# Every second weight chunk of the recurrent mixers: remainder by a negated copy on ScalarE and an accumulating DMA from GpSimd, in place of a subtraction on VectorE

## The chip, the cores and the metric

The kernel runs on one core of one Trainium2 chip. The metric is the device time of one execution in microseconds (us). Of each kernel several executions are timed; one more is recorded by the profiler, and all views below are of that one. Engine names in the views: PE is TensorE, PEld its weight loads, DVE VectorE, ACT ScalarE, POOL GpSimd, SP the engine that issues most DMAs.

## What is computed

256 tokens of width 1024, in float32, go through two layers of a first block and one of a second block. A layer of the first block is a feed-forward network, a recurrent mixer, and another feed-forward network. The mixer, cut to what matters:

```
proj = (h @ w_in)                          # 1024 x 3592, in fp32 accuracy
hg_q, hg_f, hg_i, hg_g, gd_q, gd_k, gd_v, gd_z, gd_b, gd_a, rg_x, rg_gate = split(proj)
o_hg = hgrn2_chunked(q, 1.0 - f, hg_i, log(f))          # 4 heads
o_gd = gated_delta_chunked(cq, ck, cv, g, beta)         # 4 heads, a triangular solve per 128 tokens
o_rg = rg_lru(causal_depthwise_conv(rg_x)) * gelu(rg_gate)
x = x + concat(o_hg, o_gd, o_rg) @ w_out                # 1024 x 1024
```

The feed-forward networks are `(silu(h @ w_gate) * (h @ w_up)) @ w_down` with an inner width of 2816. The second block has retention, dilated attention and a third feed-forward part.

## The kernel before

**Weights in two parts.** Every matrix product is done in three matmuls of type float32r, on a high part and a remainder of both operands: high by high, high by remainder, remainder by high. The function `wchunk` brings a weight chunk of at most 256 x 512 numbers into the form [128 partitions, 2, n]: a DMA on SP's queue writes it to `raw`, ScalarE copies it to `wh` (a cast, L92), and VectorE subtracts `wh` from `raw` and writes the remainder `wl` (L93). The pool of `raw` has 4 buffers and that of `wh` and `wl` 3 each. So a load into a `raw` buffer waits until the subtraction four chunks earlier is done, and a cast waits until the matmuls of the chunk three earlier are done.

**Who reads the chunks.** `gemm_feat` (output features on partitions) uses a chunk in 24 matmuls with lines L184 (`wh` by the high part), L185 (`wh` by the remainder) and L186 (`wl`). `gemm_tok` uses one in 12 matmuls, with lines L140, L141 (`wl`) and L142. PE takes its instructions in the order in which they stand: a matmul on `wl` that is not there yet holds up all that stand behind it.

**The mixer.** `Mixer` runs twice (mixer 0 and mixer 1). It projects in the order rg, ba, k, hg, vg, v, q, z, 4 chunks each, and its last step `project` has 8 chunks of `w_out`. Between these products stand the recurrences: `delta_solve` (matmuls `sv`, L711, with small steps on VectorE and ScalarE between them), `hg_scores` (matmuls `hS`, L915), `delta_core`. Here chunks are counted as the program asks for them: mixer 0 has chunks #71 to #110, mixer 1 #251 to #290. Of mixer 0, rg is #71 to #74, ba #75 to #78 (260 columns), k #79 to #82, hg #83 to #86, z #99 to #102 (260 columns) and `project` #103 to #110. The convolution after k starts with `xp` (L622).

**The order of the work.** No order is written out by hand. A scheduler of the framework puts each engine's instructions in a row when the program is built, after its own model of their times; so a change in one helper moves other instructions too. GpSimd has little to do before: it fills some tiles with zeros and makes four small copies and two larger ones.

Of the kernel before, what the change touches and what calls it, by code (L numbers as in the profile page):

```python
# [7 lines left out]
F32 = mybir.dt.float32  # L8
# [3 lines left out]
ALU = mybir.AluOpType  # L12
# [11 lines left out]
class Weights:  # L24
# [3 lines left out]
    def __init__(self, dram, size):  # L28
        self.dram, self.size, self.parts, self.off = dram, size, [], 0
# [22 lines left out]
class Ctx:  # L52


    def __init__(self, tc, stack):
        self.tc = tc
        self.nc = tc.nc
        pool = lambda name, bufs, **k: stack.enter_context(tc.tile_pool(name=name, bufs=bufs, **k))
        self.const = pool("const", 1)
        self.keep = pool("keep", 1)  # L60
        self.raw = pool("raw", 4)
        self.wsp = pool("wsp", 3)
        self.w2p = pool("w2", 11)
        self.small = pool("small", 2)
        self.ps_mm = pool("ps_mm", 4, space=bass.MemoryType.PSUM)
        self.ps_x = pool("ps_x", 2, space=bass.MemoryType.PSUM)
        self.m4 = pool("m4", 3)
        self.rowp = pool("rowp", 2)
        self.ret = pool("ret", 4)
        self.n = 0  # L70
        self.nx = 0
        self.xtags = ("xa", "xb")
        nc = self.nc
        self.ones = self.const.tile([P, P], F32, name="ones")
        nc.vector.memset(self.ones, 1.0)
        self.ident = self.const.tile([P, P], F32, name="ident")
        nc.gpsimd.affine_select(self.ident, self.ones, pattern=[[-1, P]], compare_op=ALU.is_equal,
                                fill=0.0, base=0, channel_multiplier=1)
# [6 lines left out]
    def wchunk(self, w, k0, nkt, c0, n, room=None):  # L85
        nc = self.nc
        raw = self.raw.tile([P, KC, 512], F32, tag="raw", name=self.nm("raw"))[:, :nkt, :n]
        nc.sync.dma_start(raw, w.chunk(k0, nkt, c0, n))
        if room is None:
            room = tuple(self.wsp.tile([P, KC, 512], F32R, tag=i, name=self.nm(i)) for i in ("wh", "wl"))  # L90
        h, l = (a[:, :nkt, :n] for a in room)
        nc.scalar.copy(h, raw)  # L92
        nc.vector.tensor_tensor(l, raw, h.bitcast(F32), op=ALU.subtract)  # L93
        return h, l

    def mm_tile(self, name="mm"):
# [199 lines left out]
def hidden_split(c, hT, hc, f0, nb):  # L296

    k0 = f0 // P
    h, l = hT[k0 // 8]
    k0 %= 8  # L300
    c.split(h[:, k0:k0 + nb], l[:, k0:k0 + nb], hc)


def ffn(c, st, wT, wg, wu, wd, F):


    nc = c.nc
    xs, r = st.norm_T(wT)
    rbc = r_broadcast(c, r)
    rq = c.small.tile([P, 2], F32, tag="rr", name=c.nm("rr"))  # L310
    nc.vector.tensor_scalar(rq, r, 0.25, None, op0=ALU.mult)
    KF = F // P
    hT = [c.hT_tile(j) for j in range((KF + 7) // 8)]
    rb = bc(rbc.unsqueeze(1), [P, 2, S])
    for c0 in range(0, F, 512):
        n = min(512, F - c0)
        g = c.gemm_feat(xs, wg, 8, c0, n)
        gs = []
        for i in range(n // 256):
            gn, th = v2(c.w2("gn"), 2), v2(c.w2("th"), 2)  # L320
            nc.vector.tensor_tensor(gn, v2(g[i], 2), rb, op=ALU.mult)
            nc.scalar.activation(th, gn, AF.Tanh, scale=0.5)
            nc.vector.scalar_tensor_tensor(th, th, 1.0, gn, op0=ALU.add, op1=ALU.mult)
            gs.append(th)
        u = c.gemm_feat(xs, wu, 8, c0, n)
        for i in range(n // 256):
            nc.vector.tensor_tensor(gs[i], gs[i], v2(u[i], 2), op=ALU.mult)
            hidden_split(c, hT, gs[i], c0 + 256 * i, 2)
    for c0 in (0, 512):
        o = c.gemm_tok(hT, wd, 0, KF, c0, 512)  # L330
        for t in range(2):
            xx = st.x[:, t, c0:c0 + 512]
            nc.vector.scalar_tensor_tensor(xx, o[t], rq[:, t:t + 1], xx, op0=ALU.mult, op1=ALU.add)
# [40 lines left out]
def bc(ap, shape):  # L374
    return ap.broadcast_to(list(shape))
# [29 lines left out]
def load_cols(c, col, layout):  # L405
    t = c.const.tile([P, col.shape[1]], F32, name="colp")
    c.nc.scalar.dma_start(t, col)
    return {k: t[:, o:o + w] for k, (o, w) in layout.items()}
# [53 lines left out]
def load_consts(c, tab):  # L462
    t = c.keep.tile([P, CTAB], F32, tag="ctab", name="ctab")[:, :CONST_TAB.shape[1]]
    c.nc.sync.dma_start(t, tab)
    c.K = {n: t[:, o:o + w] for n, (o, w) in CONST_LAYOUT.items()}
    c.K["ident"] = c.ident
    c.seg = c.const.tile([P, 4, P], F32, name="seg")
    c.nc.vector.memset(c.seg, 1.0)
    c.nc.vector.memset(c.seg[:, :, 0:1], 0.0)


def r_broadcast(c, r):

    nc = c.nc
    ps = c.x_tile("rbc")
    for t in range(2):
        dg = c.small.tile([P, P], F32, tag="dg", name=c.nm("dg"))
        nc.vector.tensor_scalar(dg, c.ident, r[:, t:t + 1], None, op0=ALU.mult)
        nc.tensor.matmul(ps[:, t * P:(t + 1) * P], c.ones, dg, start=True, stop=True)
    o = c.small.tile([P, S], F32, tag="rbcs", name=c.nm("rbcs"))  # L480
    nc.scalar.copy(o, ps[:, :S])
    return o


def v2(ap, a):
    return ap.rearrange("p (a b) -> p a b", a=a)
# [967 lines left out]
def block_kernel(tc, a, layout):  # L1454
    with ExitStack() as stack:
        c = Ctx(tc, stack)
        nc = c.nc
        st = Stream(c, a["x"])
        cols = load_cols(c, a["col"], layout)
        for L in range(2):  # L1460
            wn = lambda n: cols[n][:, 8 * L:8 * L + 8]
            ffn(c, st, wn("norm_ffn1"), a["ffn1_gate"][L], a["ffn1_up"][L], a["ffn1_down"][L], D_FF)
            if L == 0:
                load_consts(c, a["tab"])
                prm = MixParams(c, cols, a, a)
                fq = c.const.tile([P, 9], F32, name="fq")
                o = TAB2_LAYOUT["invf"][0]
                nc.sync.dma_start(fq, a["tab2"][:, o:o + 9])
                rope = Rope(c, a["pos_row"], a["pos_col"], fq[:, 0:1], fq[:, 1:9])
            Mixer(c, st, prm, a["w_in"][L], a["w_out"][L], L)  # L1470
            ffn(c, st, wn("norm_ffn2"), a["ffn2_gate"][L], a["ffn2_up"][L], a["ffn2_down"][L], D_FF)
        Block2(c, st, prm, a, rope)

# [40 lines left out]
```

## Time and profile before

| what | value |
|---|---|
| time, median of 3 runs | 1794.52 us (1789.35 to 1795.16) |
| the profiled execution: its time, its span | 1796.44 us, 1794.7 us |
| mean granted clock of TensorE | 0.981 |
| busy over the span: PE, DVE, ACT, POOL | 1734.5, 1207.1, 892.3, 13.4 us |

The profiled execution's time is 1.7 us over its span, and 1.9 us over the median of the runs. PE is busy 97% of the span, but a busy PE can be one that runs at a lower clock; the granted clock of a stretch says so. VectorE's share is not even over the span: it is highest in the two mixers, from about 197 to 386 us and from about 766 to 947 us.

### The profile page before, as it was taken

The numbers are of one execution on the slowest core, as the hardware profiler recorded it, in microseconds if no ns is written. First come the engines' busy times: TensorE is split into PE (matmuls) and PEld (weight loads), VectorE is DVE, ScalarE is ACT, GpSimd is POOL, SyncE is SP. The second block draws the span as 40 slices with busy tenths as digits, with TensorE's granted clock in tenths as the row PEclk, the third lists the DMA queues.
The fourth block names the chain that finished last, engine by engine and source line by source line (L and its number), as shares of the span: only waits on it lengthen the run. The fifth ranks groups of instructions, "written<-read, shape, count | busy, mean of one in ns | idle before, by whom it ended". The sixth has DMA issues, their size and how long they took to land.

```text
span 1794.7 us, 28677 instructions
## 1 busy us (share of the span) xinstructions
PE 1734.5 (97%) x11296; PEld 1568.8 (87%) x11296; DVE 1207.1 (67%) x2181; ACT 892.3 (50%) x1352; POOL 13.4 (1%) x40
## 2 busy tenths in 40 slices
PE   8999989989999999989889999999999999999996
PEld 8997989879998999889879998888888788799885
DVE  6666689866655665589967665745666666766566
ACT  5444574444444444466345444555454544455454
POOL 0000000000000000000000000000000000000000
PEclk9999999899999999999989999999999999999998
DMA  6546542235565555543315556555443456645561
GB/s 233 186 153 220 163 135 84 94 104 185 176 197 189 183 188 181 186 151 118 127 47 177 187 169 199 185 176 173 133 130 124 146 176 211 200 155 198 194 229 53
DMA packets 91654, 292.38 MB, mean 163 GB/s; under 512 B 11008, under 2 KB 23808, under 8 KB 91520
## 3 DMA queue, kind: packets, MB, share of 16 engines
q1 hardware_dynamic: 91376, 290.45, 49.4%
q8 instruction: 88, 1.44, 0.3%
q14 instruction: 46, 0.38, 0.1%
q10 hardware_dynamic: 144, 0.11, 0.0%
HBM read 289.47 MB, written 1.05 MB: 162 GB/s over the span
## 4 chain that ended last, share of the span: by engine, by line
PE 90%; DVE 6%; ACT 2%; issue 1%; DMA 1%; SPq 0%; DVEq 0%; ACTq 0%
PE mm L185 13%; PE mm L186 13%; PE mm L184 13%; PE mm L140 13%; PE mm L141 13%; PE mm L142 13%; PE sv L711 2%; DVE wl L93 1%; ACT wh L92 1%; PE pv L1234 1%; PE dS L658 1%; PE dsc L1202 1%; PE hS L915 1%; PE dsc L1201 0%; DVE cv L630 0%
## 5 line engine op out<-in xcount | busy, mean ns | idle before, releaser
L93 DVE TENSOR_TENSOR wl<-raw,wh 128x1024 fp32r<-128x1024 f32 (+2 forms) x544 | 639.8, 1177 | 462.8 <-ACT wh L92 461.4
L92 ACT CAST wh<-raw 128x1024 fp32r<-128x1024 f32 (+2 forms) x544 | 549.3, 1011 | 652.1 <-PE mm L185 281.0
L184 PE MATMUL mm<-xTh,wh 128*128 128x256 f32 x2112 | 595.6, 284 | 13.1 <-DVE xp L622 10.0
L185 PE MATMUL mm<-xTl,wh 128*128 128x256 f32 x2112 | 598.0, 284 | 2.2 <-DVE xTl L197 2.1
L186 PE MATMUL mm<-xTh,wl 128*128 128x256 f32 x2112 | 595.2, 283 | 0.8 <-DVE wl L93 0.7
L184 PEld LDWEIGHTS mm<-xTh,wh 128*128 128x128 f32 x2112 | 401.4, 191 | 17.9 <-ACT th L572 10.4
L185 PEld LDWEIGHTS mm<-xTl,wh 128*128 128x128 f32 x2112 | 402.5, 191 | 4.7 <-DVE xTl L197 3.7
L186 PEld LDWEIGHTS mm<-xTh,wl 128*128 128x128 f32 x2112 | 403.0, 191 | 2.8 <-DVE wl L93 1.3
L141 PE MATMUL mm<-wl,hT 128*128 128x512 f32 x608 | 241.4, 398 | 2.4 <-DVE wl L93 2.4
L142 PE MATMUL mm<-wh,hT 128*128 128x512 f32 x608 | 238.8, 394 | 0.0
L140 PE MATMUL mm<-wh,hT 128*128 128x512 f32 x608 | 219.3, 397 | 4.8 <-DVE scr L573 4.8
L141 PE MATMUL mm<-wl,xTh 128*128 128x512 f32 (+1 forms) x440 | 169.3, 386 | 0.0
L142 PE MATMUL mm<-wh,xTl 128*128 128x512 f32 (+1 forms) x440 | 166.2, 380 | 0.0
L140 PE MATMUL mm<-wh,xTh 128*128 128x512 f32 (+1 forms) x440 | 160.2, 384 | 2.5 <-ACT xTh L196 2.5
L140 PEld LDWEIGHTS mm<-wh,hT 128*128 128x128 f32 x608 | 114.9, 190 | 30.2 <-DVE scr L573 5.2
L141 PEld LDWEIGHTS mm<-wl,hT 128*128 128x128 f32 x608 | 115.4, 190 | 28.3 <-DVE wl L93 3.9
L142 PEld LDWEIGHTS mm<-wh,hT 128*128 128x128 f32 x608 | 115.2, 189 | 24.7 <-DVE hT L197 0.2
L140 PEld LDWEIGHTS mm<-wh,xTh 128*128 128x128 f32 x440 | 82.0, 188 | 19.0 <-ACT xTh L196 2.9
L142 PEld LDWEIGHTS mm<-wh,xTl 128*128 128x128 f32 x440 | 83.0, 189 | 16.6 <-issue 2.0
L141 PEld LDWEIGHTS mm<-wl,xTh 128*128 128x128 f32 x440 | 82.9, 188 | 16.2 <-issue 1.9
L196 ACT ACTIVATE xTh<-xtr,colp 128x256 fp32r<-128x256 f32 (+1 forms) x72 | 28.9, 453 | 12.4 <-DVE xTl L197 12.3
L711 PE MATMUL sv<-hS,LTm 128*128 128x32 f32 x192 | 27.5, 293 | 7.3 <-ACT hS L732 4.3
(441 smaller groups left out, 1608.2 us busy)
## 6 DMA issues: line engine op xcount, KB each, us to landing
raw<-in_weights SPq DMA_DIRECT2D x514, 512.0 KB, 3.3
raw<-in_weights SPq DMA_DIRECT2D x32, 256.0 KB, 3.1
raw<-in_weights SPq DMA_DIRECT2D x16, 260.0 KB, 3.1
x_res<-in_x SPq DMA_DIRECT2D x2, 512.0 KB, 4.3
rowp<-in_b_gate SPq DMA_DIRECT2D x2, 512.0 KB, 4.8
out<-pg SPq DMA_DIRECT2D x4, 256.0 KB, 2.1
tab<-in_tab SPq DMA_DIRECT2D x1, 900.5 KB, 5.1
ctab<-in_tab SPq DMA_DIRECT2D x1, 900.0 KB, 9.7
```

The lines of the kernel that those rows point to most:

```text
L92: nc.scalar.copy(h, raw)
L93: nc.vector.tensor_tensor(l, raw, h.bitcast(F32), op=ALU.subtract)
L140: nc.tensor.matmul(o, xh[:, kt, tok], wh[:, k], start=a and k == 0, stop=False)
L141: nc.tensor.matmul(o, xh[:, kt, tok], wl[:, k], start=False, stop=False)
L142: nc.tensor.matmul(o, xl[:, kt, tok], wh[:, k], start=False, stop=z and k == m - 1)
L184: nc.tensor.matmul(o, wh[:, k, cs], xh[:, kt], start=a, stop=False)
L185: nc.tensor.matmul(o, wh[:, k, cs], xl[:, kt], start=False, stop=False)
L186: nc.tensor.matmul(o, wl[:, k, cs], xh[:, kt], start=False, stop=z)
L196: nc.scalar.activation(h, src, AF.Copy, scale=scale)
L658: nc.tensor.matmul(ps[:, h], k[:, h, sb * P:(sb + 1) * P], src[:, h, tb * P:(tb + 1) * P], start=True, stop=True)
L711: nc.tensor.matmul(o[:, h], lhsT[:, h], rhs[:, h], start=True, stop=True)
L915: nc.tensor.matmul(ps[:, i], B[:, j, t * P:(t + 1) * P], Q[:, i].rearrange("p h t -> p (h t)"), start=True, stop=True)
```

## The change

While a mixer is built, a flag is set, and every chunk with an odd count makes its remainder in another way. ScalarE writes the negative of `wh` into `wl`, and GpSimd issues a DMA that adds `raw` to `wl` in place. Chunks with an even count, and all chunks outside the mixers, keep the subtraction on VectorE.

```diff
@@ Ctx.__init__
+        self.nw, self.dma_rest = 0, False
@@ Ctx.wchunk
         nc.scalar.copy(h, raw)
-        nc.vector.tensor_tensor(l, raw, h.bitcast(F32), op=ALU.subtract)
+        self.nw += 1
+        if self.dma_rest and self.nw % 2:
+            nc.scalar.mul(l, h.bitcast(F32), -1.0)
+            nc.gpsimd.dma_start(l, raw, accum_op=ALU.add)
+        else:
+            nc.vector.tensor_tensor(l, raw, h.bitcast(F32), op=ALU.subtract)
         return h, l
@@ block_kernel
+            c.dma_rest = True
             Mixer(c, st, prm, a["w_in"][L], a["w_out"][L], L)
+            c.dma_rest = False
```

That is 20 chunks of each mixer, 40 in all: 16 of 128x1024 and 4 of 128x520 in each. The scheduler's order is the same up to the first of them. Line numbers are up to 8 higher behind the change. Three places of the new order follow.

ScalarE, at the end of the projection k in mixer 0. `wh_2552` before and `wh_2557` now are the cast of chunk #81; `rth` and `spe` are small steps of the gates. Before:

```order
L92 CAST wh_2552<-raw_2550 128x1024
L588 ACT_TABLE_LOAD
L588 ACTIVATE beta_2641<-ab_2479 128x8
L92 CAST wh_2582<-raw_2580 128x1024
L975 ACTIVATE rth_346_2370<-rgg_2369,hb 128x256
L975 ACTIVATE rth_348_2376<-rgg_2375,hb 128x256
L400 ACTIVATE spe_2644<-spe_2644 128x8
L92 CAST wh_2870<-raw_2868 128x1024
```

And now:

```order
L93 CAST wh_2557<-raw_2555 128x1024
L981 ACTIVATE rth_346_2372<-rgg_2371,hb 128x256
L594 ACTIVATE beta_2647<-ab_2483 128x8
L981 ACTIVATE rth_348_2378<-rgg_2377,hb 128x256
L406 ACTIVATE spe_2650<-spe_2650 128x8
L96 ACTIVATE wl_2558<-wh_2557 128x1024
L988 ACTIVATE ra_2385<-rth_346_2372 128x512
L989 ACTIVATE rtl_2386<-rth_346_2372 128x512
L93 CAST wh_2588<-raw_2586 128x1024
```

The negative copy of #81 (`wl_2558`) stands behind four steps of the gates, the last of which (`spe`) needs the products of ba; the cast of #82 has moved behind it.

GpSimd, from the start of mixer 0. `scr`, `rxp` and `xp` are fills with zeros. Before:

```order
L716 COPY hS_2229<-ctab 128x128
L870 MEMSET scr_2227 128x512
L958 MEMSET rxp_2354 128x2x3
L621 MEMSET xp_2611 128x2x3
L621 MEMSET xp_2622 128x2x3
```

And now:

```order
L722 COPY hS_2229<-ctab 128x128
L97 DMA wl_2237<-raw_2234 128x1024
L876 MEMSET scr_2227 128x512
L964 MEMSET rxp_2356 128x2x3
L97 DMA wl_2298<-raw_2295 128x1024
L97 DMA wl_2412<-raw_2409 128x2x260
L97 DMA wl_2449<-raw_2446 128x2x260
L97 DMA wl_2497<-raw_2494 128x1024
L97 DMA wl_2558<-raw_2555 128x1024
L97 DMA wl_2877<-raw_2874 128x1024
L627 MEMSET xp_2617 128x2x3
L627 MEMSET xp_2628 128x2x3
```

The accumulating DMAs of #71, #73, #75, #77, #79, #81 and #83 stand in GpSimd's row among the fills; each waits there for ScalarE's negative copy, and what stands behind it waits too.

PE, in the last step `project` of mixer 0. `wh_3999` before and `wh_4018` now are chunk #109, with its remainders `wl_4000` and `wl_4019`; `wh_3981` is #108 before and #107 now, `wh_3963` #107 before and `wh_4000` #108 now. Before:

```order
L140 MATMUL mm_3885<-wh_3999,hT_2222 128x512
L140 MATMUL mm_3886<-wh_3963,hT_2222 128x512
L141 MATMUL mm_3886<-wl_3964,hT_2222 128x512
L140 MATMUL mm_3888<-wh_3981,hT_2222 128x512
L141 MATMUL mm_3888<-wl_3982,hT_2222 128x512
L141 MATMUL mm_3885<-wl_4000,hT_2222 128x512
```

And now:

```order
L146 MATMUL mm_3901<-wh_4018,hT_2222 128x512
L146 MATMUL mm_3902<-wh_3981,hT_2222 128x512
L147 MATMUL mm_3902<-wl_3982,hT_2222 128x512
L146 MATMUL mm_3904<-wh_4000,hT_2222 128x512
L147 MATMUL mm_3904<-wl_4001,hT_2222 128x512
L148 MATMUL mm_3902<-wh_3981,hT_2223 128x512
L146 MATMUL mm_3902<-wh_3981,hT_2222 128x512
L147 MATMUL mm_3902<-wl_3982,hT_2222 128x512
L148 MATMUL mm_3902<-wh_3981,hT_2223 128x512
L148 MATMUL mm_3904<-wh_4000,hT_2223 128x512
L146 MATMUL mm_3904<-wh_4000,hT_2222 128x512
L147 MATMUL mm_3904<-wl_4001,hT_2222 128x512
```

Behind these twelve rows stand one more on `wh_4000` and one on `wh_4018`, and only then the first on `wl_4019`. So 13 matmuls stand between the first on #109's high part and the first on its remainder, where 4 did before.

## Rows read from the trace of the kernel before

**Rows 1.** The page's first line: the span of the profiled execution.

```profile
span 1794.7 us, 28677 instructions
```

**Rows 2.** Windows over mixer 0 and mixer 1: length, then busy us of PE, PEld, DVE, ACT, POOL, granted clock.

```profile
206.00:386.00 180.00, 165.38 (x1177) 156.00 (x1176) 153.87 (x357) 95.04 (x174) 4.97 (x15) 0.93 0.32 103
767.00:947.00 180.00, 164.24 (x1181) 154.08 (x1179) 155.56 (x361) 95.38 (x177) 2.89 (x11) 0.93 0.35 112
```

**Rows 3.** Windows of 10 us in mixer 0, same columns.

```profile
230.00:240.00 10.00, 5.03 (x43) 4.86 (x42) 9.06 (x24) 8.66 (x13) 0.17 (x2) 0.99 0.51 168
240.00:250.00 10.00, 10.00 (x75) 10.00 (x75) 10.00 (x27) 5.47 (x9) 0.00 (x0) 0.84 0.04 11
...
270.00:280.00 10.00, 7.51 (x37) 6.92 (x36) 9.90 (x19) 4.48 (x7) 0.00 (x0) 0.70 0.33 111
```

**Rows 4.** The window of mixer 0's middle part, same columns.

```profile
240.00:350.00 110.00, 104.65 (x747) 100.25 (x747) 103.31 (x231) 55.37 (x107) 4.27 (x12) 0.89 0.27 88
```

**Rows 5.** Who waited for whom in mixer 0: us in total, times, longest.

```profile
PE mm L184 <- DVE xp L622: 5.0, 1, 5.0
```

**Rows 6.** Groups of mixer 0 by line and form: count, busy us, mean ns, idle before.

```profile
L93 DVE TENSOR_TENSOR wl<-raw,wh 128x1024 fp32r<-128x1024 f32 x32 | 38.8, 1219 | 7.9 <-ACT wh L92 7.8
...
L93 DVE TENSOR_TENSOR wl<-raw,wh 128x520 fp32r<-128x520 f32 x8 | 5.6, 695 | 1.4 <-ACT wh L92 1.4
```

**Rows 7.** The same view for ACT.

```profile
L92 ACT CAST wh<-raw 128x1024 fp32r<-128x1024 f32 x31 | 32.1, 1046 | 21.3 <-PE mm L185 9.4 <-PE mm L142 9.1 <-issue 1.7
...
L92 ACT CAST wh<-raw 128x520 fp32r<-128x520 f32 x8 | 5.0, 627 | 8.4 <-issue 4.1 <-PE mm L185 4.0 <-PE mm L142 0.3
...
L675 ACT ACTIVATE scr<-scr,cs 128x128 f32<-128x128 f32 x12 | 3.6, 387 | 0.0
...
L196 ACT ACTIVATE hT<-yT,colp 128x512 fp32r<-128x512 f32 x2 | 1.4, 690 | 0.3 <-PE yT L813 0.3
```

**Rows 8.** DMA issues of the whole program: count, KB each, median us to landing.

```profile
raw<-in_weights SPq DMA_DIRECT2D x514, 512.0 KB, 3.3
...
raw<-in_weights SPq DMA_DIRECT2D x16, 260.0 KB, 3.1
...
tab<-in_tab SPq DMA_DIRECT2D x1, 900.5 KB, 5.1
ctab<-in_tab SPq DMA_DIRECT2D x1, 900.0 KB, 9.7
```

**Rows 9.** Timeline of ACT in mixer 0: start us, length us, then the instruction.

```profile
197.79 1.05 ACT L92 CAST wh<-raw 128x1024 fp32r<-128x1024 f32 x1 [0.61 <-PE mm L142]
...
216.37 0.63 ACT L92 CAST wh<-raw 128x520 fp32r<-128x520 f32 x1 [0.97 <-PE mm L185]
...
227.42 0.21 ACT L400 ACTIVATE spe<-spe 128x8 f32<-128x8 f32 x1 [0.62 <-DVE spe L399]
...
270.15 1.98 ACT L92 CAST wh<-raw 128x1024 fp32r<-128x1024 f32 x2
...
374.23 1.04 ACT L92 CAST wh<-raw 128x1024 fp32r<-128x1024 f32 x1
```

**Rows 10.** Timeline of PE: first matmuls on remainders of #71, #77, #81, #91, #109.

```profile
203.56 0.28 PE L186 MATMUL mm<-xTh,wl 128*128 128x256 f32 x1
...
218.76 0.28 PE L141 MATMUL mm<-wl,xTh 128*128 128x260 f32 x1
...
228.83 0.47 PE L186 MATMUL mm<-xTh,wl 128*128 128x256 f32 x1
...
275.06 0.58 PE L186 MATMUL mm<-xTh,wl 128*128 128x256 f32 x1
...
378.18 0.62 PE L141 MATMUL mm<-wl,hT 128*128 128x512 f32 x2
```

**Rows 11.** The chain that ended last, before `xp` in mixer 0: start us, us, what.

```profile
229.23 1.23 DVE wl L93
...
236.35 1.23 DVE wl L93
```

## The prediction

> **What bounds the kernel now.** I read the span first [rows 1], then the windows over the two mixers, since the change touches nothing else. Each is 180 us long, with PE busy 165.38 and 164.24 us at a granted clock of 0.93, and VectorE busy 153.87 and 155.56 us [rows 2]. The two are copies of each other, so I work one out and double it.
>
> Inside mixer 0 the windows of 10 us tell three parts apart. At the front (197 to 240 us) PE runs the products rg, ba and k one after the other and is the bound; then it stands idle for 5.0 us, waiting for VectorE's `xp` [rows 5], within a window that shows it busy for 5.03 of 10, and the next window runs at a clock of 0.84 [rows 3]. In the middle (240 to 350 us) VectorE is busy 103.31 of 110 us; PE is busy 104.65, but at a clock of 0.89 [rows 4], because its short pauses cost it the clock: 2.5 idle us in one window go with a clock of 0.70 [rows 3]. The reader should see two engines that are both nearly full there, and that VectorE is the slightly tighter one. At the end (350 to 386 us) PE runs `project` and VectorE has time to spare.
>
> **What is removed.** 16 subtractions of 1219 ns and 4 of 695 ns per mixer [rows 6]: 22.3 us of VectorE's time. Ten of them (#87 to #105, two of the short form) stand in the middle: 8 x 1.22 + 2 x 0.70 = 11.2 us.
>
> **What is added.** On ScalarE, 16 negative copies and 4 short ones. The trace has none of this kind; the cast of the same tile takes 1046 and 627 ns [rows 7], and I take that: 19.2 us per mixer. ScalarE is busy 95.04 of 180 us [rows 2], so it has room; but it takes its instructions in order.
>
> On GpSimd and the DMA queues, 20 transfers. Nothing in the trace accumulates and nothing is issued by GpSimd, so I bound the time X from ScalarE's copy to the landing. From below: a load of the same 512 KB lands 3.3 us after its issue [rows 8]. From above: an accumulate reads the destination as well as the source, so its data is nearer to the 900 KB of the table loads, which took 5.1 and 9.7 us [rows 8]. I take 5.5 us for the large form, the quicker table load with some contention, and 4 us for the short one, which with both operands is a 512 KB load with some more. Both ends, 3.3 and 9.7, go into the range.
>
> So a changed chunk's remainder is there 1.05 + 5.5 = 6.6 us after its cast has ended, where the subtraction took 1.2. Whether that costs anything depends on the lead, from the cast's end to the first matmul on the remainder. PE takes matmuls in order and reaches the remainder half a microsecond after it starts on a chunk, so all that lies beyond the lead is a stall.
>
> **The front.** #71: cast from 197.79, 1.05 long [rows 9], first used at 203.56 [rows 10]. New: 197.79 + 1.05 + 1.05 + 5.5 = 205.39, a stall of 1.8 us. #77: its cast starts at 216.37 [rows 9] because its buffer comes free then, so it moves with the stall, to 218.2; ready at 218.2 + 0.63 + 0.63 + 4 = 223.5; used before at 218.76 [rows 10], now at 220.6 plus four matmuls that the new order puts ahead (six chunks of 12 or 24 matmuls take 15.2 us here, so 0.1 each and 0.5), so 2.4 us. #81: in the new order its copy stands behind `spe`, which was at 227.42 [rows 9]. That moves by 4.2 of stalls and back by 2.1, for two subtractions of 1.22 that no longer stand ahead of it on VectorE and a short step of 0.3 that now does: 229.5. Ready at 229.5 + 0.2 + 1.05 + 5.5 = 236.3; used at 228.83 [rows 10] + 4.2 = 233.0; 3.3 us. Together 7.5 us. The 5.0 us in which PE waited for `xp` [rows 5] take up that much, for the chain before `xp` loses two subtractions of 1.23 us [rows 11] and gains one copy of 1.05, and is not later. Front: +2.5. With X = 3.3 (3 for the short form) the stalls are 0, 1.4 and 1.0, all absorbed, and `xp` comes 2.5 - 1.05 = 1.4 earlier: -1.4. With X = 9.7 each of the three grows by 4.2: 7.5 + 12.6 - 5.0 = +15.
>
> The same delay holds a `raw` buffer longer, and SP's later loads wait for it in order. A buffer's round is then 3.3 of load, 1.05, 1.05 and 5.5, which is 10.9 us over four chunks; from #71 to #77 PE took 15.2 us for six chunks [rows 10], 10.1 for four. At X = 5.5 with its stalls that is about even; at 9.7 it is part of the +15.
>
> **The middle.** 11.2 us leave an engine that is busy 94% of this part. I take half, 5.5, because PE is nearly full too; the least is 0, the most 9. Against it stands #91: cast from 270.15 [rows 9], used at 275.06 [rows 10], a lead of 3.9 us; in the new order twelve steps of 387 ns [rows 7] come between its cast and its copy, while the cast itself comes earlier. About 2.5 us of stall, and 0.5 for the other short leads; most leads there are longer than 6.6 us and hide the transfer. Middle: -2.5; -9 with X = 3.3, +6 with 9.7.
>
> **The end.** #109: cast from 374.23 [rows 9], used as the second of the pair at 378.18, so at 378.4 [rows 10]. New: 374.23 + 1.05, 0.69 for a split that stands ahead [rows 7], 1.05 and 5.5, so 382.5; the new order has 13 matmuls instead of 4 ahead of its remainder (two that overlap take 0.62 us, so over 0.2 each and 2.1 together), at 380.5. A stall of 2 us, and 1 for the copies that now stand ahead of other steps on ScalarE: +3 (+0.5 and +7 at the ends).
>
> **The clock.** A pause of 5.0 us cost 0.16 x 10 = 1.6 us in the next window, one of 2.5 cost 3.0 [rows 3]. Three new stalls of 2 to 3 us at a mixer: +1.5 (0 to 2).
>
> **Sum.** +2.5 - 2.5 + 3 + 1.5 = +4.5 us a mixer, +9 in all. The profiled execution took 1796.4 us, so 1805; it lay 1.9 over the median of the runs, and against that I predict 1804. At the ends: 2 x (-1.4 - 9 + 0.5) = -20, so 1775; 2 x (15 + 6 + 7 + 2) = +60, so 1854.
>
> **The rivals.**
>
> Rival 1, the transfer is quick: X near 3.3, as a load of the same bytes [rows 8]. Then no stall is left over that the idle 5.0 us don't take up, and VectorE's relief decides: 1775 to 1788. The point from which it decides is X of about 4.3, where front and end come to nothing. For it speaks that VectorE is the tighter engine in the middle. Against it: a second operand must be read. The Trainium skill, page "DMA: Bandwidth & Descriptors", section "Anatomy of one DMA", gives about 2.0 us and the bytes at 436 GB/s for a DMA that GpSimd issues; that is an estimate of 3.2 us for 512 KB, and the sum by it would be this rival's. The page does not say that this holds for an accumulate.
>
> Rival 2, the transfer is slow: X of 8 to 10, as the slower table load [rows 8], because it shares the DMA engines with up to four loads that wait in SP's queue. Then the front pays fully: 1825 to 1854.
>
> Rival 3, GpSimd's issue is held up by VectorE, which is busy 94% of the middle [rows 4]. If each transfer had to wait for one step of VectorE of 0.7 us, as the short subtraction [rows 6], the five or so short leads of a mixer would add 3.5 us, 7 in all: 1811. The Trainium skill, page "SBUF — State Buffer", section "SBUF: two separate sides", says that GpSimd cannot write descriptors while VectorE runs in a two-port mode. No row here can show it, as GpSimd issues no DMA before.
>
> Rival 4, it changes nothing: relief and stalls cancel to within 5 us. 0.3% of the time, 5.4 us, is about what a measurement of this kernel can tell from no change.
>
> **Chances.** My forecast with rival 3 (slower, 1800 to 1820): 0.46. Rival 1: 0.27. Rival 2: 0.12. Rival 4: 0.15. About a tenth of the first lies within 0.3%, and as much of rival 1. Faster by over 0.3%: 0.25; within: 0.21; slower: 0.54. The range 1783 to 1838 leaves out the outer halves of rivals 1 and 2.
>
> **What would show it.** Right: VectorE's busy time falls by about 44 us, ScalarE's rises by 38, and PE's wait for `xp` is replaced by waits for a DMA that wrote `wl`, at #71, #77, #81 and #109 and their like in mixer 1; the accumulating DMA lands 5 to 6 us after issue. Wrong: landings near 3 us with PE busy through the front (rival 1), or near 9 us with SP's loads waiting for `raw` (rival 2). What would overturn the whole sum is the new order: the scheduler moved most of the middle's steps, and a solve that now ends some microseconds earlier or later counts as much as a transfer.

## The result and the profile after

The changed kernel takes 1817.44 us (median of 4 runs, 1810.16 to 1822.52), the kernel before 1794.84 (4 runs, 1789.35 to 1795.93). The ratio is 1.0121, with a 95% interval of 1.0098 to 1.0143: slower by 22 us, where the prediction had +9. The direction and the range held; the size did not.

First the page of the changed kernel: its span, busy times, the queue that is new (packets, MB, share of 16 engines), and the lines of the chain that ended last.

```profile
span 1818.6 us, 28803 instructions
...
PE 1736.9 (96%) x11296; PEld 1567.1 (86%) x11296; DVE 1167.0 (64%) x2141; ACT 926.1 (51%) x1392; POOL 52.0 (3%) x80
...
q0 software_dynamic: 6784, 18.91, 5.9%
...
PE mm L147 12%; PE mm L148 11%; PE mm L146 11%; PE mm L191 10%; PE mm L192 10%; PE mm L190 9%; DMA wl<-raw 2%; PE pv L1240 1%; PE dsc L1208 1%; PE sv L717 1%; DMA raw<-in_weights 0%; PE dsc L1207 0%; PE dpT L1226 0%; ACT wh L93 0%; DVE xTl L203 0%
```

VectorE gave up 40 us of 1207 (forecast 44) and ScalarE took on 34 (38). PE's busy time grew by only 2.4 us (1734.5 before), so 21.5 of the 24 us by which the span grew are idle time of PE, and the chain now runs through `DMA wl<-raw`.

The groups by line and form of the new kind answer to [rows 6, 7]:

```profile
L97 POOL DMA_DIRECT2D wl<-raw x40 | 37.2, 930 | 827.9 <-ACT wl L96 714.4 <-PE LZ L773 20.1 <-DVE cv L636 17.3
L96 ACT ACTIVATE wl<-wh 128x1024 fp32r<-128x1024 f32 x32 | 33.8, 1056 | 0.4
...
L96 ACT ACTIVATE wl<-wh 128x520 fp32r<-128x520 f32 x8 | 5.1, 634 | 0.1
```

The DMA issues answer to [rows 8]:

```profile
wl<-raw POOLq DMA_DIRECT2D x32, 512.0 KB, 5.3
...
wl<-raw POOLq DMA_DIRECT2D x8, 260.0 KB, 4.0
```

The copy costs what the cast costs, and the landing is 5.3 and 4.0 us after the issue, which itself comes 0.3 us behind the copy's end; I had taken 5.5 and 4 from the copy's end. The prices were right. The waits of PE (us in total, times, longest) show where they were paid: neither of the first two lines has a match before, and the third was 5.0 us in mixer 0 alone [rows 5] and 10.0 us in both mixers.

```profile
PE mm L192 <- DMA wl<-raw: 20.5, 11, 5.4
PE mm L147 <- DMA wl<-raw: 17.7, 10, 4.5
...
PE mm L190 <- DVE xp L628: 0.8, 1, 0.8
```

The window of mixer 0 from the first matmul of #71 to the last of #110, in the kernel before (same columns as [rows 2]; behind the granted clock stand the DMA share and GB/s):

```profile
203.09:386.03 182.94, 168.32 (x1201) 158.93 (x1200) 155.79 (x359) 97.95 (x179) 5.54 (x17) 0.93 0.32 103
```

The same window in the changed kernel:

```profile
199.94:396.63 196.69, 170.76 (x1199) 157.77 (x1198) 137.97 (x341) 113.97 (x198) 23.82 (x36) 0.94 0.56 147
```

The mixer is 13.75 us longer. PE's idle time (length less busy) goes from 14.6 to 25.9 us, its busy time is up by 2.4, and the granted clock of the mixer as a whole is no lower. By the same three parts as in the prediction, cut at the first matmuls of #83 and #104 in the timeline and at #110's last:

| part | forecast, a mixer | mixer 0 | mixer 1 |
|---|---|---|---|
| front | +2.5 | +3.5 | +8.4 |
| middle | -2.5 | +4.9 | +5.4 |
| end | +3 | +5.3 | -0.5 |
| clock, named by itself | +1.5 | (within the parts) | (within the parts) |

The middle has the wrong sign in both mixers. Two other parts grew by busy time of PE as well, at a lower granted clock. Here are mixer 0's end and mixer 1's front in the kernel before:

```profile
367.85:386.00 18.15, 18.15 (x84) 14.53 (x85) 12.10 (x28) 7.54 (x11) 0.53 (x1) 1.00 0.25 85
...
763.82:800.03 36.21, 31.16 (x261) 30.78 (x260) 30.25 (x78) 24.09 (x40) 0.74 (x4) 0.99 0.56 175
```

And in the changed kernel:

```profile
373.10:396.60 23.50, 21.28 (x82) 16.64 (x83) 12.06 (x28) 8.48 (x12) 1.38 (x2) 0.85 0.37 112
...
774.97:819.55 44.58, 37.44 (x266) 35.92 (x264) 25.25 (x75) 28.24 (x45) 6.57 (x10) 0.89 0.74 185
```

The middles run at 0.94 in the changed kernel, after 0.91 and 0.92, and take PE 3.6 us less busy time. In all, PE is busy 6.1 us longer in the two mixers and 3.7 us less elsewhere.

What stands in the middle are four long gaps: the timeline of PE at the first use of #91, #103, #271 and #285 (start, length, in brackets the idle time before and what ended it).

```profile
276.64 0.58 PE L192 MATMUL mm<-xTh,wl 128*128 128x256 f32 x1 [5.41 <-DMA wl<-raw]
...
339.20 0.59 PE L147 MATMUL mm<-wl,hT 128*128 128x512 f32 x1 [4.26 <-DMA wl<-raw]
...
857.03 0.58 PE L192 MATMUL mm<-xTh,wl 128*128 128x256 f32 x1 [5.25 <-DMA wl<-raw]
...
931.19 0.80 PE L147 MATMUL mm<-wl,hT 128*128 128x512 f32 x1 [4.51 <-DMA wl<-raw]
```

And the timeline of ACT ahead of the first of them:

```profile
265.31 1.05 ACT L93 CAST wh<-raw 128x1024 fp32r<-128x1024 f32 x1 [0.47 <-PE mm L148]
267.21 3.62 ACT L681 ACTIVATE scr<-scr,cs 128x128 f32<-128x128 f32 x12 [0.85 <-DVE cs L677]
270.74 1.04 ACT L96 ACTIVATE wl<-wh 128x1024 fp32r<-128x1024 f32 x1
```

#91's cast has ended at 266.36, but the copy starts behind the twelve steps at 270.74, and PE already stands at 271.23 (its first use was at 275.06 before [rows 10]). #271 is its copy in mixer 1. #103 had 17 us before between the end of its remainder and its first use; in the new order it stands right behind #102, and PE is there at 334.94, 3.8 us after the cast has ended (331.13).

#285 is another matter. PE comes to it at 926.68, 9.1 us after its cast has ended (917.56), which the forecast's 6.6 would have covered. But its transfer, issued at 920.35, lands after 10.8 us. The windows of 2 us before that landing (busy times as in [rows 2], then granted clock, DMA share, GB/s) show the DMA engines full, and SP had issued two weight loads at 919.79 and a load of 900 KB, `tab`, at 922.23:

```profile
924.00:926.00 2.00, 2.00 (x21) 2.00 (x19) 1.62 (x3) 1.25 (x5) 0.19 (x1) 1.00 1.02 253
926.00:928.00 2.00, 0.68 (x7) 0.56 (x6) 1.21 (x3) 0.51 (x2) 0.00 (x0) 1.00 1.01 275
928.00:930.00 2.00, 0.00 (x0) 0.00 (x0) 0.29 (x1) 0.00 (x0) 0.00 (x0) 0.99 0.90 335
```

The place repeats itself: in a second trace of the changed kernel this transfer takes 10.1 us, and as a plain one, in the same order, still 8.0. That the shared engines made it late is argued from these rows; no run here took the other loads away.

### The profile page after: what moved, and what is told of

The parts are those of the page before. It is cut to its first block, busy times and chain, and to the rows that moved or that the text cites. A ratio compares the mean times of both kernels' runs of the same rounds, so it can differ in the third digit from the quotient of the medians.

```text
span 1818.6 us, 28803 instructions
## 1 busy us (share of the span) xinstructions
PE 1736.9 (96%) x11296; PEld 1567.1 (86%) x11296; DVE 1167.0 (64%) x2141; ACT 926.1 (51%) x1392; POOL 52.0 (3%) x80
## 3 DMA queue, kind: packets, MB, share of 16 engines
q0 software_dynamic: 6784, 18.91, 5.9%
## 4 chain that ended last, share of the span: by engine, by line
PE 69%; DMA 3%; issue 3%; DVE 3%; ACT 2%; POOL 0%; DVEq 0%; POOLq 0%; ACTq 0%
PE mm L147 12%; PE mm L148 11%; PE mm L146 11%; PE mm L191 10%; PE mm L192 10%; PE mm L190 9%; DMA wl<-raw 2%; PE pv L1240 1%; PE dsc L1208 1%; PE sv L717 1%; DMA raw<-in_weights 0%; PE dsc L1207 0%; PE dpT L1226 0%; ACT wh L93 0%; DVE xTl L203 0%
## 5 line engine op out<-in xcount | busy, mean ns | idle before, releaser
L99 DVE TENSOR_TENSOR wl<-raw,wh 128x1024 fp32r<-128x1024 f32 (+2 forms) x504 | 595.6, 1182 | 470.8 <-ACT wh L93 464.2
L97 POOL DMA_DIRECT2D wl<-raw x40 | 37.2, 930 | 827.9 <-ACT wl L96 714.4
L96 ACT ACTIVATE wl<-wh 128x1024 fp32r<-128x1024 f32 (+1 forms) x40 | 38.9, 972 | 0.5
```

Of the source, the lines that this page charges most:

```text
L96: nc.scalar.mul(l, h.bitcast(F32), -1.0)
L97: nc.gpsimd.dma_start(l, raw, accum_op=ALU.add)
```

## The experiments

**Theory A** says that PE's waits for the landing make the loss. The rivals: **B**, the scheduler's new order costs it whatever the landing; **C**, ScalarE's 40 extra copies delay its casts; **D**, the transfers hold `raw` and `wl` longer or take bandwidth from the loads. All ratios are to the kernel before in runs on the same chip, with 95% intervals; 0.1% is 1.8 us. The framework's scheduler gave each of these kernels an order of its own, except where I say that the order is the same to the instruction.

### The landing taken away or made shorter

**Copies without transfers.**

```diff
             nc.scalar.mul(l, h.bitcast(F32), -1.0)
-            nc.gpsimd.dma_start(l, raw, accum_op=ALU.add)
```

> The negative copies on ScalarE and the new order stay, the transfers are left out, so the remainder of every second chunk is only minus the rounded weight (that part of the computation is left out). Theory A (PE waits for the landing, 38 us of such waits in the trace of the change, where the lead is short): these waits go, VectorE's relief of some 45 us stays, so 1775 to 1788 us, 0.990 to 0.996 of before. Theory B (the new order of the steps costs the time, whatever the landing): 1805 to 1820 us, 1.006 to 1.014. Theory C (ScalarE's 40 extra copies delay its casts): no faster than before, 1790 to 1800.

Measured: 1790.37 us, ratio 0.9977 (0.9959 to 0.9995). The loss is gone, but only 4 us of gain are left, just outside the range of theory A. As far as two kernels with two orders can be compared, theory C explains no more than the 4 us by which the next one, without the copies, is faster.

**No remainder at all.**

```diff
-            nc.scalar.mul(l, h.bitcast(F32), -1.0)
-            nc.gpsimd.dma_start(l, raw, accum_op=ALU.add)
+            l = h
```

> Every second chunk uses its rounded weight in place of the remainder: no subtraction, no copy, no transfer (that part of the computation is left out). It is VectorE's relief alone, with an order of its own. Theory A: 1770 to 1786 us, and at most 5 us below the kernel that keeps the copies. Theory B (order): as the kernel with the copies, above 1800. Theory C (ScalarE's copies): 10 us or more below the kernel with the copies.

Measured: 1789.86 us, 0.9956 (0.9942 to 0.9971). With VectorE relieved at no price whatever, both mixers give 8 us, less than theory A's range had. The prediction had put 11 us on the relief (5.5 a mixer), and 18 at most. The 8 us hold for this kernel's order and are no strict bound for another.

**Plain transfers, the order the same to the instruction.**

```diff
-            nc.gpsimd.dma_start(l, raw, accum_op=ALU.add)
+            nc.gpsimd.dma_start(l, raw)
```

> The same transfers at the same places, but overwriting in place of accumulating, so the remainder is the raw weight (that part of the computation is left out). What the accumulation adds to the landing: if a plain transfer of 512 KB from SBUF to SBUF by GpSimd lands 3.3 us after its issue as the loads of before do, 2 us are taken from each of some 20 waits, 38 us of PE's waits become about 10, and the time falls to some 1790 to 1800 us, 0.998 to 1.003. If it is the issue and the bytes and not the accumulation, it lands at 5 us and the time stays 1810 to 1820, 1.009 to 1.014.

Measured: 1795.19 us, 0.9996 (0.9978 to 1.0014). Its DMA issues:

```profile
wl<-raw POOLq DMA_DIRECT2D x32, 512.0 KB, 3.4
...
wl<-raw POOLq DMA_DIRECT2D x8, 260.0 KB, 3.4
```

Its waits of PE:

```profile
PE mm L192 <- DMA wl<-raw: 12.4, 4, 5.0
...
PE mm L147 <- DMA wl<-raw: 4.8, 5, 2.0
```

This pair differs in the kind of transfer alone. The landing of 512 KB comes 1.9 us sooner, PE's waits fall from 38.2 to 17.2 us, which is 21.0, and the time by 1.25%, which is 22.5 us (the two spans differ by 18.8). So the waits are paid about one for one, and theory B cannot be what makes this loss: the same order without the late landings loses nothing. PE's other idle time (span less busy time less these waits) is 43.5 us with accumulating transfers and 46.6 with plain ones, so nothing else about the accumulating kind, such as held buffers or late loads, costs PE time in this order. The order has its part in what is left: 8.8 of the 17.2 us (I had expected about 10 in all) are waits of 3.76 and 5.04 us at #91 and #271, whose copies stand behind the twelve steps.

**The transfers without a reader.**

```diff
             nc.gpsimd.dma_start(l, raw, accum_op=ALU.add)
+            l = h
```

> All copies and accumulating transfers are made, but PE multiplies by the rounded weight in place of the remainder, so no matmul waits for a landing (the remainder is left out of the product for these chunks); the buffers are still held until the landing. Theory A (PE waits for the landing of short leads): the time falls to that of the kernel without transfers, 0.996 to 0.999. Theory D (the transfer holds raw and remainder buffers longer, so that loads and casts come late, or takes DMA bandwidth from them): most of the loss stays, 1.006 to 1.012.

Measured: 1792.58 us, 0.9971 (0.9953 to 0.9988), with the transfers landing 5.2 and 4.2 us after issue. All the traffic and all the held buffers are there, though in an order of its own, and there is no loss. Together with PE's other idle time in the plain pair this speaks against theory D.

### One part of the mixer alone

The transfer at one part's odd chunks, the subtraction elsewhere; the count starts at zero in each mixer.

```diff
-        if self.dma_rest and self.nw % 2:
+        if self.dma_rest and self.nw in (1, 3, 5, 7, 9, 11):
...
-            c.dma_rest = True
+            c.dma_rest, c.nw = True, 0
```

> The accumulating transfer at six chunks of each mixer's front alone (#71 to #81, #251 to #261). By the prediction's terms: +2.5 and up to 1.5 of clock a mixer, so +5 to +8 us, 1.003 to 1.005. By the trace of the change, whose front is 3.5 and 8.4 us longer in the two mixers: +12 us, 1.0065.

> The transfer at ten chunks of each mixer's middle alone (#83 to #101, #263 to #281). By the prediction's term, -2.5 a mixer: -5 us, 0.997. If the relief of VectorE is given back here in PE's waits (10 us longer over both mixers in the trace of the change, of which the part behind #101 belongs to chunks that this kernel leaves on VectorE): 0 to +8 us, 1.000 to 1.0045.

> The transfer at the last four odd chunks of each mixer alone (#103 to #109, #283 to #289). By the prediction's term, +3 a mixer: +6 us, 1.0035. By the trace of the change, where PE waits 4.3, 4.5 and 2.2 us for three of the four in mixer 0 and 0.7, 4.5 and 1.0 in mixer 1: +6 to +14 us, 1.0035 to 1.008. In no case faster than before.

Measured: the front alone 1.0182 (1.0165 to 1.0200), the middle alone 0.9994 (0.9979 to 1.0009), the end alone 1.0026 (1.0005 to 1.0047). The middle gains nothing (it has 9.7 us of waits at two chunks), and the end costs 5 us, about the forecast's 6. The front was a surprise: 33 us, more than the whole change, and beyond what both readings expected. Windows of its mixer 0 as a whole and of one stretch:

```profile
205.69:412.41 206.72, 192.01 (x1201) 180.59 (x1200) 150.20 (x354) 103.00 (x184) 10.71 (x22) 0.83 0.36 104
...
308.00:356.00 48.00, 48.00 (x225) 48.00 (x226) 35.23 (x81) 15.09 (x34) 1.66 (x6) 0.50 0.11 38
```

The mixer is 23.8 us longer than before, with an idle time of 14.7 us, the same as before's 14.6. All of it is busy time: for 48 us PE never pauses and runs at a granted clock of 0.50, 1.2 GHz. So the loss there is of another kind, and I asked whether the landings or the order bring it about.

**The front alone with plain transfers, the same order.** The edit is again the one word of the accumulation.

> The kernel with transfers at the front alone (1.0182), in exactly its order of instructions, but with plain transfers in place of accumulating ones (so the remainder of twelve chunks is the raw weight; that part of the computation is left out). That kernel lost 24 us in mixer 0 to a granted clock of 0.5 over a stretch of some 50 us, with no more idle time of PE than before. If its order brings that stretch about: 1.012 to 1.018, and the same stretch at 0.5. If the later landings do (about 2 us each at the front): 0.999 to 1.004, and the clock as in the kernel before.

Measured: 1819.48 us, 1.0144 (1.0119 to 1.0170). Its stretch from 298 to 345 us runs at 0.61 and waits little; PE's waits for landings are 3.1 us in the whole program, against 9.9 with accumulation. Hence of the 33 us the landings are 7 (1.0182 less 1.0144, give or take 6), about the difference of the waits, 6.8. The other 26 are there with plain transfers too, and the two kernels share the order of the instructions; by elimination they come with it. Theory B is true of this kernel, though not of the change.

```profile
298.00:345.00 47.00, 45.11 (x244) 44.78 (x242) 39.37 (x88) 14.90 (x34) 1.87 (x8) 0.61 0.19 67
```

**The middle alone with plain transfers, the same order.**

> The kernel with transfers in the middles alone (0.9994), in exactly its order of instructions, with plain transfers in place of accumulating ones (the remainder of twenty chunks is the raw weight; that part of the computation is left out). In the accumulating kernel PE waits for a landing twice, 9.7 us in all, at the chunks behind the split steps (#91, #271). If only those two short leads cost there, landings 1.5 to 2 us sooner give back 3 to 4 us: 0.997 to 0.998. If every landing of the middle costs 0.55 us as in the whole change, 20 of them give back 11 us: 0.993 to 0.994. If the order decides and not the landings: 0.999 to 1.000.

Measured: 1790.01 us, 0.9973 (0.9962 to 0.9983), against 0.9994: 4 us back, give or take 3, as expected if only the two short leads cost. Their waits shrink from 9.7 to 6.2 us in all. But in the two traces PE's idle time as a whole is the same (59.5 and 59.2 us) and its busy time is 5.1 us shorter, so that these two waits alone cost the 4 us is not shown.

### Which part of the changed kernel the waits lie in

The last set keeps the changed kernel's order to the instruction and makes one part's transfers plain, beside the changed kernel itself on the same chip.

```diff
-            nc.gpsimd.dma_start(l, raw, accum_op=ALU.add)
+            if 12 < self.nw < 36:
+                nc.gpsimd.dma_start(l, raw)
+            else:
+                nc.gpsimd.dma_start(l, raw, accum_op=ALU.add)
...
-            c.dma_rest = True
+            c.dma_rest, c.nw = True, 0
```

That is the middle; the front has `self.nw < 12` in its place, the end `self.nw > 36`.

> The changed kernel in exactly its order, with plain transfers at the front alone (#71 to #81, #251 to #261; their remainder is the raw weight, so that part of the computation is left out), accumulating ones elsewhere. By the prediction's front (three stalls of 2.5 us a mixer, of which each gives back 1.9): 7 to 11 us less than the changed kernel. By the waits in the trace of the change (4.0 and 5.9 us at the front, each wait cut by 1.9 at most): 8.6 us less.

> The same with plain transfers in the middle alone (#83 to #105, #263 to #285; their remainder is the raw weight). By the prediction's middle (#91 and 0.5 us of others, 3 us a mixer): 4 to 5 us less than the changed kernel. By the waits in its trace (11.8 and 13.2 us, each cut by 1.9 at most): 13 us less.

> The same with plain transfers at the end alone (#107, #109, #287, #289; their remainder is the raw weight). By the prediction's end (one stall of 2 us a mixer, at #109 and #289) as by the waits in the trace (2.2 and 1.0 us): 3 to 4 us less than the changed kernel.

> The changed kernel itself, as the measure for the other three on the same chip: 1.010 to 1.014 of before.

| plain at | ratio | us below the changed kernel | expected by the prediction's terms | by the waits |
|---|---|---|---|---|
| none (the change) | 1.0141 (1.0114 to 1.0168) | | | |
| front | 1.0082 (1.0057 to 1.0106) | 11 | 7 to 11 | 8.6 |
| middle | 1.0060 (1.0033 to 1.0087) | 15 | 4 to 5 | 13 |
| end | 1.0134 (1.0109 to 1.0158) | 1 | 3 to 4 | 3 to 4 |

The differences of the ratios times 1796 us give the third column; each is uncertain by about 7 us either way. The front gives what the prediction's terms had there, the middle three times that and more than its uncertainty explains. Together they give some 26 us, as do all transfers plain (0.9996, measured on another chip, less 1.0141).

### Three versions with the whole computation

**Each transfer in two halves.**

```diff
-            nc.gpsimd.dma_start(l, raw, accum_op=ALU.add)
+            for k in (0, nkt // 2):
+                nc.gpsimd.dma_start(l[:, k:k + nkt // 2], raw[:, k:k + nkt // 2], accum_op=ALU.add)
```

> Each accumulating transfer is issued as two halves of its rows of tiles (256 KB each), the computation is whole. Theory A (PE waits for the landing): the 260 KB transfers land 1.3 us sooner than those of 512 KB, so the first half is there about 1.3 us sooner and the second while PE works on the first; 40 x 0.55 us was the price of 1.9 us of landing, so some 10 to 15 us of the 22 come back: 1.004 to 1.007. If GpSimd's issue (0.93 us each) or a fixed part of each transfer decides, the second half lands as late as the whole did or later: 1.010 to 1.018.

Measured: 1823.41 us, 1.0161 (1.0131 to 1.0192); the gain that theory A had here did not come. A half of 256 KB lands 4.3 us after its issue, where the whole takes 5.3, so most of the time is no matter of bytes. PE's waits for transfers fall to 21.4 us, but 7.5 us that the view puts down to ScalarE's copies come beside them (in each of these three waits a transfer has landed only 0.1 us before the copy's end), and PE's busy time grows to 1749.3 us. The order is another one, so how much of this is the halves' own stays open.

**Long leads alone**, eight chunks of each middle:

```diff
-        if self.dma_rest and self.nw % 2:
+        if self.dma_rest and self.nw in (13, 15, 17, 19, 23, 25, 27, 29):
```

> The accumulating transfer only at the eight odd chunks of each middle that have long leads in the trace of the change (#83 to #89, #93 to #99 and their like; #91 and #101, the front and the end stay on VectorE). By the reading that only short leads cost: VectorE's relief of 8.5 us a mixer and waits of under 2 us, 0.994 to 0.998, the first kernel with the whole computation below before. If the relief is worth nothing at PE's bound, or the new order makes other leads short: 0.999 to 1.003.

Measured: 1800.98 us, 1.0029 (1.0009 to 1.0049). My reading failed here: PE waits for no landing any more, and the kernel is still no faster. These are PE's waits in its trace:

```profile
PE mm L192 <- DVE wl L99: 7.2, 2, 4.2
PE mm L190 <- DVE xp L628: 6.1, 2, 3.1
...
PE sv L717 <- DVE LTm L762: 4.3, 2, 2.2
```

PE waits for VectorE again, at subtractions that were left to it. But the profiled execution, with a span of 1791.1 us, was no slower than the kernel before, so why the median is slower stays open.

**The subtraction on GpSimd**, without copy and transfer:

```diff
-            nc.scalar.mul(l, h.bitcast(F32), -1.0)
-            nc.gpsimd.dma_start(l, raw, accum_op=ALU.add)
+            nc.gpsimd.tensor_tensor(l, raw, h.bitcast(F32), op=ALU.subtract)
```

> Every second remainder is subtracted by GpSimd itself, with no copy on ScalarE and no transfer; the computation is whole. GpSimd's other steps of this trace are short ones, so its time for 128x2048 elements is open: at twice VectorE's 1.22 us the remainder is there 2.4 us after the cast, 4 us sooner than by transfer, and the time falls to that of the kernels without landings, 0.995 to 0.998; at 6 us or more it is as late as the transfer: 1.010 or above. If GpSimd and VectorE hold each other up, VectorE's mean step grows above the 1182 ns of the trace of the change.

Measured: 1825.50 us, 1.0170 (1.0148 to 1.0192). A miss with a lesson. The groups of its trace:

```profile
L96 POOL TENSOR_TENSOR wl<-raw,wh 128x1024 fp32r<-128x1024 f32 x32 | 81.3, 2540 | 729.6 <-ACT wh L93 677.6 <-DVE gg L407 21.4 <-issue 12.3
...
L973 DVE SCALAR_TENSOR_TENSOR rxc<-rxp,colp,rxc 128x256 f32<-128x256 f32 x12 | 13.6, 1184 | 0.0
...
L592 DVE TENSOR_TENSOR gg<-gg,nea 128x4 f32<-128x4 f32 x4 | 5.0, 1278 | 0.1
```

GpSimd's 2540 ns are near the 2.4 us under which I expected a gain. But VectorE's whole busy time is 1213.1 us, against 1166.0 in the kernel with the copies alone, for the same 2141 instructions: the first of these steps takes 475 ns there and 1184 here, the second 156 and 1278. What GpSimd takes over, VectorE pays back in steps that run beside it.

None of the versions with the whole computation beats the kernel before.

## Why the prediction was right in direction and wrong in size

**The transfer and the copy: right.** 5.3 and 4.0 us from issue to landing, 1056 and 634 ns for the copies.

**The front: right in the places, by luck in the size.** I named #71, #77 and #81. PE waits 1.27, 1.40 and 1.21 us there in mixer 0 (forecast 1.8, 2.4, 3.3), and 1.09, 1.34 and 3.18 at their like in mixer 1; the 5.0 us of waiting for `xp` [rows 5] fell to 0.8, so they were taken up as said. By these two the fronts would be about even. They are 3.5 and 8.4 us longer because PE's busy time there grew too, by 1.9 and 6.3 us, the latter at a granted clock of 0.89 after 0.99. Plain transfers at the front give back 11 us, the upper end of what the forecast's stalls would.

**The middle: the step that failed.** The prediction said: "most leads there are longer than 6.6 us and hide the transfer. Middle: -2.5". It had 3 us of stalls a mixer; the trace has 11.8 and 13.2 us of waits (#83 to #105, #263 to #285), and plain transfers there give back 15 us where the forecast's stalls would have given 4 to 5. 13 of the 24 transfers there cost PE no wait. But I had read the leads from the timeline of before, and in the new order some are short. At #91 and #271 I had the twelve steps on ScalarE, but PE comes to #91 at 271.23 and not at 275.06 (5.41 and 5.25 us of wait, forecast 2.5 each). #103, which had 17 us before and so was no part of my sum, waits 4.26. #285 has the lead, but meets a landing twice as long as the median (4.51). All nine that wait besides #91 and #271 make 14.4 us, where I had 1.

**The relief: too large.** Half of VectorE's 11.2 us a mixer was to come back as time, 11 us in all. PE's idle time that is no wait for a landing fell from 60.2 to 43.5 us, which is 16.7; `xp` is 9.2 of it, and the other 7.5 are what the trace shows of the relief. The kernel with no remainder (8 us) and the one with the copies alone (4 us) point the same way, each in its own order.

**The end: about right in the waits.** #109 waits 2.18 us (forecast 2.0), #289 1.02. In mixer 0 PE is also busy 3.1 us longer there, at a clock of 0.85 after 1.00. Plain transfers there give back 1 us, too little to tell from none.

**The clock: right in kind, not in the place.** PE's busy time grew by 6.1 us in the mixers and 2.4 over the whole program, where I had 3. Behind the waits at #103 and #109 the granted clock falls to 0.50, 1.2 GHz:

```profile
339.50:342.90 3.40, 3.40 (x9) 2.64 (x8) 1.39 (x3) 1.30 (x3) 0.31 (x1) 0.50 0.77 177
390.70:394.10 3.40, 3.40 (x9) 2.62 (x9) 1.19 (x2) 0.45 (x1) 0.00 (x0) 0.50 0.97 347
```

That the middles run at a higher clock than before was no part of my sum, and makes up for a part of this.

So, over both mixers: the forecast had 25 us of waits for landings (front 15, middle 6, end 4), 5 of other costs (clock 3, copies at the end 2), and 21 that come back (`xp` 10, relief 11), which gives 9. The traces have 38.2 us of waits (9.9, 25.0 and 3.2), 2.4 of busy time, and 16.7 that came back, which gives the 23.9 by which the span grew. The middle's waits were 19 us too few, the front's 5 too many, and 4 us too much was to come back.

**The rivals.** Rival 1, the quick transfer, is what the plain transfers made real, with landings at 3.4 us: 1775 to 1788 us was its forecast, and the time came out as before, 1795: even with quick landings 17.2 us of waits stay, where its sum had only a few, all taken up by `xp`. The Trainium skill, page "DMA: Bandwidth & Descriptors", section "Anatomy of one DMA", has the fit from which the prediction took 3.2 us; the plain transfer's 3.4 agrees with it, and the accumulating one's 5.3 shows that it does not hold for that kind. Rival 2, landings of 8 us and more, did not come about as a median, but its mechanism, other loads on the same DMA engines, fits the landing of 10.8 us at #285 (the next longest of the 40 are 9.5 and 8.0). Of rival 3, GpSimd held up by VectorE, the issues show nothing: all 40 start 0.3 us behind the copy's end and take 0.85 to 1.20 us. Rival 4 falls with the result.

What stays open: why the scheduler's orders differ so in worth. That the order brings some 26 us in the kernel with the front alone follows from the plain pair; which of its moves does is not shown. In the changed kernel the order cannot be told apart from the relief, and why the kernel with long leads alone is not faster is not known.

## What to carry to other kernels

A longer way to the same operand costs nothing while its lead is long, so list the leads of every moved chunk; but read them in the order of the changed program, since a scheduler moves the steps that made them. A few of them decide: four gaps of 4 to 5 us here made half of all waits. Before trading work away from an engine, gauge the relief by a version that drops the work: here 0.4%, less than a third of the 26 us that the transfers cost. And test a landing by a pair in the same order, as accumulating against plain, because a change that moves the order too can be worth more than what it was made for.

## What the runs showed of the hardware

An accumulating transfer of 512 KB from SBUF to SBUF lands 5.3 us (median) after GpSimd issues it, a plain one at the same place 3.4. It takes GpSimd 930 ns to issue against 573, and the DMA engines 5.9% of the span against 3.0% for the same 18.91 MB.

The granted clock can stay at 1.2 GHz for 48 us in which PE shows no pause: that is in the kernel with the front alone, from 308 to 356 us. The fall, at 305 us, came at the end of a wait of 1.6 us. Of the 225 matmuls of that stretch 148 are the solve's and `hS`, as the groups by line show; in the same window of the kernel before, at a clock of 0.86, these three groups have 120 of 326.

```profile
L717 PE MATMUL sv<-hS,scr 128*128 128x32 f32 x64 | 14.4, 389 | 0.0
L717 PE MATMUL sv<-hS,LTm 128*128 128x32 f32 x52 | 11.7, 387 | 0.0
L921 PE MATMUL hS<-scr,hB 128*128 128x128 f32 x32 | 8.4, 438 | 0.0
```

Two-operand steps of VectorE grow longer beside subtractions on GpSimd, in the two groups shown by 2.5 and 8 times in the mean. The Trainium skill, page "SBUF — State Buffer", section "SBUF: two separate sides", says that the two share a pair of ports which one holds for a whole instruction while the other is blocked; the trace agrees, with a mean of 1184 ns against 475.
